# Software-issued weight-sum transfers released by an attention counter, and key transposes without a holding time

## The chip, the core and the metric

The kernel runs on one core of a Trainium2 chip. The metric is the device time of one execution in microseconds (us), taken as the median of three runs. A profile of one more execution gives, for each engine, when every instruction began and how long it took. Engines are called as in the profile: PE is TensorE's matmul, PEld its weight load, DVE VectorE, ACT ScalarE, POOL GpSimd, SP SyncE. An engine with a q behind its name (SPq, POOLq) is its queue.

## What is computed

One decoder block on 512 tokens of width 1024, in float32. The input is normalised and projected into fifteen pieces; two token mixers run beside each other; their outputs are gated, merged, projected, normalised and added to the input.

```python
h = rms_norm(x, norm_pre)
proj = h @ w_in
(q_n, k_c, v_c, k_s, v_s, k_w, v_w, g_n, z_n,
 q_r, k_r, v_r, z_r, m_a, m_b) = jnp.split(proj, split_points(), axis=-1)
...
y_a = (o_a * jax.nn.silu(z_n)) @ w_nsa_o      # o_a: sparse attention, 8 heads of 64
...
y_b = (o_b * jax.nn.silu(z_r)) @ w_ret_o      # o_b: retention, 4 heads
merged = jax.nn.sigmoid(m_a) * y_a + jax.nn.sigmoid(m_b) * y_b
x = x + rms_norm(merged @ w_out, norm_post)
```

The attention has three branches with softmaxes of their own: keys compressed by a small network (`cmp_w1`, `cmp_w2`), selected keys and a sliding window.

## The kernel before

**Precision.** Every float32 operand of a large product is split into a rounded high part and the rest (`whi`, `wlo` for weights, `hTh`, `hTl` for the normalised input, `kA`, `kB` for keys), and a product is three matmuls: high by high, high by low, low by high. ACT or DVE makes the high part, DVE the low part (`sub_split`, which is a subtraction in `tt`, line 209).

**Weights.** They lie in one stream in the order of their use. SP loads them in pieces of 512 KB into four buffers `raw` (`load_next`, line 354); `splitter` makes `whi`/`wlo` halves of 512 columns from them into nine buffers; a `raw` buffer is loaded anew when both halves are split. Each piece holds two contraction steps of 128 (two "kt").

**Stages of `main`.** First the block A (the keys and values of the compressed and selected branches, 512 columns, four token tiles t at once), then block C (280 columns: window keys, values and gates; one tile after the other, eight kt of three matmuls each), then the queries Q (tiles 3, 2, 1, 0), then the two halves of the compression network (`hidden(0)`, `hidden(1)`: four pieces of weights each), then the blocks of `PLAN`, of which Z is the first (four passes over the same four pieces of weights). Attention runs between the matmuls of Q to ZR, retention between those of the blocks VR.

**What sets the order.** No queue is sorted by the hardware. The body is a set of Python generators; `Order.run` picks the next one by priority and by a clock of its own, which adds up estimated costs (`self.now` for PE, `self.eng` for the others). A generator that yields a number isn't resumed before that time on the planner's clock, one that yields a function not before the function is true. What an instruction waits for on the chip is set by its data alone: a time that was yielded is not in the program.

**Keys of block A (`tail_a`, lines 589 to 619).** For each tile t: ACT scales the product out of PSUM into `nat`; DVE turns it (`rope16`) and copies each key twice into `kd` (`doubled`, line 564, 128x768); then `keysT` makes PE transpose two 128x128 pieces of `kd` (line 234, `ident`), ACT writes `kA` and DVE `kB`; then four more transposes with `identp` feed `Xk` and `Xv` (four additions on DVE), the input of the compression network. There are two buffers for `kd`, and two PSUM banks (91 and 92) for transposes. Between the copy and `keysT` the generator yields `e + HOLD`, with HOLD 1500 ns. Block C's keys go the same way (`tail_c`, 128x256 copies, `arena_l`), without a holding time.

**Weight sums (`weight_sums`, lines 327 to 337).** The two blocks of `SEVEN` (the second halves of the gates m_a and m_b) are multiplied with seven products in place of eight, which needs sums of weight blocks. They are made in DRAM by 16 transfers of 512 KB that POOL issues through the software queue: eight copies out of the weight stream (line 334), then eight with `accum_op=OP.add` (line 336), of which the first four add from the stream and the last four add one sum to another (`t<-t`). The accumulating ones wait for the transfers that wrote their operands. The sums are read as weights from 383 us on. In the planner the k-th transfer is yielded at 110 us + k times 12 us.

**The gated products (`att_sum`, lines 920 to 942).** When the eighth part of an output (t, g) of the attention is there, the branches' sum is multiplied into `szn` by `tt(...)`, which by its default runs on DVE; then a flag `att{t}{g}` is set in the planner. Eight such flags make `ATT`.

**POOL's other work** in the middle of the kernel: four additions `gate` (one for each tile of block C), eight powers `rv` in retention (line 209), and four `rr` at the end.

Of the kernel before, what the change touches and what calls it, by code (L numbers as in the profile page):

```python
# [36 lines left out]
ISSUE = 8.0  # L37
SLACK = 700.0
WAKE = 7
HOLD = 1500.0  # L40
T0, TSTEP = 110000.0, 12000.0
DVE_BIAS = 400


# [95 lines left out]
def block_kernel(ctx: ExitStack, tc, x, xT, x0s, ws, small, w2s, norm_post, rope_r, dmask, out):  # L140
# [19 lines left out]
    def at(kb, n, dt=FT):  # L160
        o = int(kb * 256)
        if dt == FR:
            return arena_r[:, o:o + n]
        assert o >= 28 * 256 or o + n <= 28 * 256
        return arena_f[:, o - 28 * 256:o - 28 * 256 + n] if o >= 28 * 256 else arena_l[:, o:o + n]
# [30 lines left out]
    def act(o, i, func=AF.Copy, r=0.0, **kw):  # L196
        S.activation(o, i, func, **kw)  # L197
        return od.op("act", act_ns(o, i, lazy(kw.get("bias"), kw.get("scale"))) + (95 if "accum_out" in kw else 0), r)
# [9 lines left out]
    def tt(o, a, b, op, r=0.0, e="dve"):  # L208
        (V if e == "dve" else G).tensor_tensor(o, a, b, op=op)  # L209
        if op == OP.pow:  # L210
            return od.op(e, 300 + 164 * size(o), r, True)
        return od.op(e, (1.042 * size(o) + 69) if e == "dve" else (2.36 * size(o) + 77), r, e == "pool" or near(o, a, b))
# [20 lines left out]
    def tr(ps, a, idn, r=0.0):  # L233
        T.transpose(ps, a, idn)  # L234
        return od.pe(86 if a.dtype == FR else 108, r, 45.0 if a.dtype == FR else 31.0)
# [75 lines left out]


    loads, off = [], 0
    sums = []
    for pieces in stream_shape():
        if pieces == "seven":
            b11, b12, b21, b22 = (ws[off + i * P * 1024:off + (i + 1) * P * 1024].rearrange("(p n) -> p n", p=P)
# [9 lines left out]
    def weight_sums():  # L327

        for n in range(8):
            for i, block in enumerate(sums):  # L330
                yield T0 + TSTEP * (n * len(sums) + i)
                o, a = block[n]
                if n < 4:
                    G.dma_start(o, a)
                else:
                    G.dma_start(o, a, accum_op=OP.add)
                od.op("pool", 900.0)
# [186 lines left out]
    def rs(t, i=0):  # L524
        return rs3[:, i, t:t + 1]
# [16 lines left out]
    def rope16(v, t, shape, r, e="dve"):  # L542

        n = int(np.prod(shape))
        pat = {1: "p (a c) -> p a c", 2: "p (a b c) -> p a b c"}[len(shape)]
        kw = dict(zip("ab", shape))
        t1, t2 = (at(41 + 0.5 * i, n * 16).rearrange(pat, **kw) for i in range(2))

        def bc(a):
            c = a.shape[-1]  # L550
            for _ in shape:
                a = a.unsqueeze(1)
            return a.broadcast_to([P, *shape, c])
        ix = (slice(None),) * (1 + len(shape))
        lo, hi, al = ix + (slice(0, 8),), ix + (slice(8, 16),), ix + (slice(0, 16),)
        tt(t1, v[al], bc(ropen[:, t, 0:16]), OP.mult, r, e)
        tt(t2[lo], v[hi], bc(ropen[:, t, 16:24]), OP.mult, r, e)
        r = tt(t2[hi], v[lo], bc(ropen[:, t, 24:32]), OP.mult, r, e)
        return tt(v[al], t1, t2, OP.add, r, e)

    def doubled(kn, a, b, kd, r):

        n = (b - a) // 64
        V.tensor_copy(kd.rearrange("p (a r c) -> p a r c", a=n, r=2),
                      kn[:, a:b].rearrange("p (a c) -> p a c", c=64).unsqueeze(2).broadcast_to([P, n, 2, 64]))
        return od.op("dve", 0.53 * n * P + 70, r, True)

    def keysT(kd, off, br, t, r):
        ps = yield from PT.get()
        yield r + PE_LAG  # L570
        for g in range(2):
            e = tr(ps[:, g * P:(g + 1) * P], kd[:, off + g * P:off + (g + 1) * P], ident, r)
        yield e, "act"
        v = ps[:, 0:256].rearrange("p (g c) -> p g c", g=2)
        sl = (slice(None), br, slice(None), slice(t * P, (t + 1) * P))
        e = act(kA[sl], v, r=e)
        yield e, "dve"
        e = sub_split(kB[sl], v, kA[sl], e)
        PT.put(ps, e)
        return e  # L580

    def vals(src, br, t, r):
        for g in range(2):
            sv = src[:, g * 64:(g + 1) * 64]
            e = act(VS[:, t, br, g, g, :], sv, r=r)
            e = sub_split(VS[:, t, br, g, 1 - g, :], sv, VS[:, t, br, g, g, :], e)
        return e

    def tail_a(t, ps, e, ring):
        yield od.need("const", "rs")  # L590
        kn = yield from NAT.get()
        yield max(e, constr["rope"], rsr[0]), "act"
        e = act(kn, ps, r=e, scale=rs(t))
        ring.put(ps, e)
        yield e, "dve"
        v = kn.rearrange("p (b e) -> p b e", b=2)[:, :, 0:128].rearrange("p b (g c) -> p b g c", g=2)
        e = rope16(v, t, (2, 2), e)
        kd = yield from KD6.get()
        e = doubled(kn, 0, 384, kd, e)
        ev = vals(kn[:, 384:512], 0, t, 0.0)  # L600
        NAT.put(kn, ev)
        yield e + HOLD
        yield from keysT(kd, 512, 0, t, e)
        pc = yield from PT.get()
        yield e + PE_LAG
        for i in range(4):
            ep = tr(pc[:, i * P:(i + 1) * P], kd[:, i * P:(i + 1) * P], identp, e)
        KD6.put(kd, ep)
        yield ep, "dve"
        for i, X in enumerate((Xk, Xv)):  # L610
            src = pc[:, i * 256:(i + 1) * 256].rearrange("p (g l c) -> p g l c", g=2, l=16)
            for hf in range(2):
                rr = slice(hf * 64, hf * 64 + 64)
                c0 = 8 * t - hf
                lo = 1 if c0 < 0 else 0
                o = X[rr, :, :, c0 + lo:c0 + 8].rearrange("p l g c -> p g l c")
                ep = tt(o, src[rr, :, :, lo:8],
                        pes[i][rr, :].unsqueeze(1).unsqueeze(3).broadcast_to([64, 2, 16, 8 - lo]), OP.add, ep)
        PT.put(pc, ep)
        od.flags.add(f"A{t}")  # L620
# [291 lines left out]
    def att_out():  # L912
        for t, g in ((t, g) for t in reversed(range(NT)) for g in range(2)):
            yield lambda: (t, g) in avs
            a = avs[t, g]
            po = yield from PO.get()
            a["po"] = po
            od.spawn(att_sum(t, g, po), 1)

    def att_sum(t, g, po):  # L920
        a = avs[t, g]
        yield lambda: a["n"] == a["total"]
        yield od.need("Z0", "Z1", "Z2", "Z3")
        m, o = slice(g * 64, g * 64 + 64), slice(64 - g * 64, 128 - g * 64)
        low = yield from NAT.get()
        yield a["e"], "act"
        e = act(low[m], po[o], r=a["e"])
        yield e, "dve"
        e = tt(low[m], po[m], low[m], OP.add, e)
        PO.put(po, e)  # L930
        yield e, "pool"
        gv = szn[m, :, t * P:(t + 1) * P]
        e = tt(gv, low[m].rearrange("p (j c) -> p j c", j=4), gv, OP.mult, e)
        NAT.put(low, e)
        od.flags.add(f"att{t}{g}")
        if all(n in od.flags for n in ATT):
            DMA.dma_start(dm, dmask.rearrange("h p c -> p h c"))
            dmr.append(od.dma(P * 2048, a["e"]))
            for o in (32, 36):
                VR[0].put((at(o, 512, FR), at(o + 2, 512, FR)))  # L940
            for _ in range(2):
                b = yield from PO.get()
                PS.put(b)
# [530 lines left out]
    od.spawn(splitter(), lambda: rank(nxt[0])())  # L1474
    od.spawn(edges(), 1)
    od.spawn(weight_sums(), 1)
    od.spawn(main(), MAIN)
    od.run()
# [28 lines left out]
def stream_shape():  # L1507

    yield [512, 512]
    yield from [[1024]] * 3  # L1510
    yield from [[560]] * 4
    yield from [[1024]] * (4 + 8)
    for b in PLAN:
        yield from ["seven"] if b in SEVEN else [[1024]] * (2 if b[0] == "NO" else 4)
    yield from [[1024]] * 8
# [67 lines left out]
```

## Time and profile before

| | |
|---|---|
| median of three runs | 528.15 us (527.85 to 531.55) |
| profiled execution, its own time | 528.24 us |
| its span, first to last instruction | 526.5 us |
| mean granted clock of PE | 0.997 |
| PE busy | 514.9 us (98% of the span) |
| DVE, ACT, POOL busy | 405.6, 290.5, 23.8 us |
| read, written in HBM | 66.26 MB, 10.49 MB |

The span has 1.7 us less than the time of that execution. Matmuls overlap: one of 512 columns is shown with some 0.39 us, and the next one starts 0.23 us behind it. So starts are compared here, and not durations. A row of the timeline gives the start, the duration, the engine and line, what was done, and in brackets the idle time ahead of it with what ended that. In the list of transfers the last column is the time from issue to landing.

### The profile page before, as it was taken

The numbers are of one execution on the slowest core, as the hardware profiler recorded it, in microseconds if no ns is written. First come the engines' busy times: TensorE is split into PE (matmuls) and PEld (weight loads), VectorE is DVE, ScalarE is ACT, GpSimd is POOL, SyncE is SP. The second block draws the span as 40 slices with busy tenths as digits, with TensorE's granted clock in tenths as the row PEclk, the third lists the DMA queues.
The fourth block names the chain that finished last, engine by engine and source line by source line (L and its number), as shares of the span: only waits on it lengthen the run. The fifth ranks groups of instructions, "written<-read, shape, count | busy, mean of one in ns | idle before, by whom it ended". The sixth has DMA issues, their size and how long they took to land.

```text
span 526.5 us, 7843 instructions
## 1 busy us (share of the span) xinstructions
PE 514.9 (98%) x2778; PEld 440.8 (84%) x2778; DVE 405.6 (77%) x980; ACT 290.5 (55%) x627; POOL 23.8 (5%) x48
## 2 busy tenths in 40 slices
PE   8989999999999999999999999999999999999995
PEld 7888888788888888888878888888788989988884
DVE  6698799989979889997886576786889867645533
ACT  6663798768557886784525353524557434323411
POOL 1002100000000000000111000000000000000000
PEclk9999999999999999999999999999999999999998
DMA  8956769601304004133543532141643726625032
GB/s 311 365 198 200 220 132 260 209 2 40 121 1 129 33 0 156 36 112 119 109 136 66 190 125 76 41 120 42 219 141 122 237 83 202 205 114 159 1 109 92
DMA packets 22456, 68.87 MB, mean 131 GB/s; under 512 B 2448, under 2 KB 3728, under 8 KB 22416
## 3 DMA queue, kind: packets, MB, share of 16 engines
q1 hardware_dynamic: 19968, 59.84, 33.9%
q0 software_dynamic: 2304, 8.39, 7.2%
q8 instruction: 22, 0.36, 0.3%
q10 hardware_dynamic: 144, 0.14, 0.1%
q14 instruction: 18, 0.15, 0.1%
HBM read 66.26 MB, written 10.49 MB: 146 GB/s over the span
## 4 chain that ended last, share of the span: by engine, by line
PE 81%; DVE 7%; DMA 7%; issue 2%; ACT 1%; SPq 1%; POOLq 0%; DVEq 0%; POOL 0%; ACTq 0%
PE bank L230 76%; DMA raw<-in_stream_dram 6%; PE bank L234 6%; DVE wlo L209 3%; DVE arena_r L209 1%; DMA arena_f<-in_xT_dram 1%; DVE arena_l L844 1%; DVE arena_f L209 1%; DVE arena_l L218 1%; ACT whi L197 0%; DVE nat L209 0%; ACT arena_l L197 0%; DVE whi L205 0%; SPq L477 0%; DVE arena_f L222 0%
## 5 line engine op out<-in xcount | busy, mean ns | idle before, releaser
L197 ACT ACTIVATE whi<-raw 128x512 fp32r<-128x512 f32 x159 | 95.7, 626 | 41.3 <-PE bank L230 32.2
L209 DVE TENSOR_TENSOR wlo<-raw,whi 128x512 fp32r<-128x512 f32 x172 | 111.7, 685 | 7.6 <-ACT whi L197 6.8
L230 PE MATMUL bank<-whi,hTh 128*128 128x512 f32 x256 | 99.7, 405 | 0.8 <-DVE arena_r L222 0.4
L230 PE MATMUL bank<-whi,hTl 128*128 128x512 f32 x256 | 96.2, 391 | 0.0
L230 PE MATMUL bank<-wlo,hTh 128*128 128x512 f32 x256 | 96.1, 391 | 0.0
L230 PE MATMUL bank<-arena_r 128*128 128x256 f32 (+2 forms) x328 | 70.7, 336 | 0.3 <-DVE arena_r L209 0.3
L230 PE MATMUL bank<-arena_r,whi 128*128 128x512 f32 (+1 forms) x208 | 63.8, 382 | 0.7 <-DVE sg L222 0.7
L197 ACT ACTIVATE arena_r<-bank 128x512 fp32r<-128x512 f32 (+2 forms) x80 | 45.2, 570 | 29.1 <-PE bank L234 27.7
L197 ACT ACTIVATE arena_l<-arena_l,stat 128x128 f32<-128x128 f32 (+3 forms) x104 | 55.3, 552 | 5.6 <-DVE stat L209 2.7
L209 DVE TENSOR_TENSOR arena_r<-bank,arena_r 128x512 fp32r<-128x512 f32 (+2 forms) x72 | 46.8, 656 | 13.8 <-ACT arena_r L197 13.1
L230 PEld LDWEIGHTS bank<-whi,hTl 128*128 128x128 f32 x256 | 48.0, 188 | 10.6
L230 PEld LDWEIGHTS bank<-arena_r 128*128 128x128 f32 x328 | 51.0, 189 | 6.5 <-DVE arena_r L209 0.6
L230 PEld LDWEIGHTS bank<-whi,hTh 128*128 128x128 f32 x256 | 48.0, 188 | 9.5 <-DVE arena_r L222 0.9
L230 PEld LDWEIGHTS bank<-wlo,hTh 128*128 128x128 f32 x256 | 48.3, 189 | 8.2
L230 PE MATMUL bank<-hTh,whi 128*128 128x512 f32 (+1 forms) x144 | 52.4, 364 | 0.0
L230 PE MATMUL bank<-hTh,wlo 128*128 128x512 f32 (+1 forms) x144 | 51.2, 355 | 0.0
L230 PE MATMUL bank<-hTl,whi 128*128 128x512 f32 (+1 forms) x144 | 51.1, 355 | 0.0
L230 PE MATMUL bank<-whi,arena_r 128*128 128x512 f32 (+1 forms) x176 | 48.7, 352 | 0.0
L230 PEld LDWEIGHTS bank<-arena_r,whi 128*128 128x128 f32 x208 | 38.8, 188 | 8.6 <-DVE sg L222 1.3
L230 PE MATMUL bank<-arena_r,wlo 128*128 128x512 f32 x96 | 37.4, 389 | 0.0
L230 PEld LDWEIGHTS bank<-whi,arena_r 128*128 128x128 f32 x176 | 32.1, 189 | 4.6
L230 PE MATMUL bank<-wlo,arena_r 128*128 128x512 f32 (+1 forms) x104 | 34.7, 343 | 0.3 <-DVE wlo L209 0.3
(164 smaller groups left out, 768.4 us busy)
## 6 DMA issues: line engine op xcount, KB each, us to landing
raw<-in_stream_dram SPq DMA_DIRECT2D x77, 512.0 KB, 4.3
t<-in_stream_dram POOLq DMA_DIRECT2D x12, 512.0 KB, 5.3
raw<-t SPq DMA_DIRECT2D x8, 512.0 KB, 3.7
arena_f<-in_rope_r_dram SPq DMA_DIRECT2D x8, 256.0 KB, 2.7
t<-t POOLq DMA_DIRECT2D x4, 512.0 KB, 5.4
arena_f<-in_xT_dram SPq DMA_DIRECT2D x8, 256.0 KB, 3.7
ends<-in_x_dram SPq DMA_DIRECT2D x4, 512.0 KB, 5.5
arena_l<-in_xT_dram SPq DMA_DIRECT2D x7, 256.0 KB, 5.7
```

Source lines behind the costliest of these rows:

```text
L197: S.activation(o, i, func, **kw)
L209: (V if e == "dve" else G).tensor_tensor(o, a, b, op=op)
L218: V.tensor_scalar(o, a, s1, s2, op0=op0, op1=op1)
L230: T.matmul(ps, a, b, start=start, stop=stop)
L234: T.transpose(ps, a, idn)
L844: V.tensor_tensor_reduce(pv[:, b, :], sv[:, b, :], maskp[:, 512 - L:512], 1.0, -NEG, OP.add, OP.min, nm[:, b:b + 1])
```

## The change

It has two parts. The times at which the planner releases the 16 software transfers are replaced by a counter: transfer k is released when k is below twice the number of finished outputs of the attention (`PER = 2`; eight outputs release 16 transfers). And the holding time between the copy of block A's keys and their transposes is dropped.

```diff
-HOLD = 1500.0
-T0, TSTEP = 110000.0, 12000.0
+PER = 2
...
-    sums = []
+    sums, atts = [], [0]
...
         for n in range(8):
             for i, block in enumerate(sums):
-                yield T0 + TSTEP * (n * len(sums) + i)
+                while (n * len(sums) + i) >= PER * atts[0]:
+                    yield lambda: (n * len(sums) + i) < PER * atts[0]
                 o, a = block[n]
                 if n < 4:
                     G.dma_start(o, a)
...
         ev = vals(kn[:, 384:512], 0, t, 0.0)
         NAT.put(kn, ev)
-        yield e + HOLD
         yield from keysT(kd, 512, 0, t, e)
...
         od.flags.add(f"att{t}{g}")
+        atts[0] += 1
```

No instruction is added or removed: PE has 2051 rows in the order of both, POOL the same 16 transfers, four additions and twelve powers. What moves is their order. Lines of the changed kernel are one lower from line 42 to 328 and from 603 to 935, so lines 229, 233 and 208 there are 230, 234 and 209 before.

**POOL behind the first eight transfers.** `t_115` to `t_122` are the eight sums in DRAM, `rv` are retention's powers. Before:

```order
L336 DMA t_115<-in_stream_dram 128x1024
L336 DMA t_119<-in_stream_dram 128x1024
L336 DMA t_117<-in_stream_dram 128x1024
L336 DMA t_121<-in_stream_dram 128x1024
L209 TENSOR_TENSOR rv<-rv,nhalf 128x2
L336 DMA t_116<-t_117 128x1024
L209 TENSOR_TENSOR rv<-rv,nhalf 128x2
L336 DMA t_120<-t_121 128x1024
L209 TENSOR_TENSOR rv<-rv,nhalf 128x2
L336 DMA t_118<-t_116 128x1024
L209 TENSOR_TENSOR rv<-rv,nhalf 128x2
L336 DMA t_122<-t_120 128x1024
```

The changed kernel:

```order
L336 DMA t_115<-in_stream_dram 128x1024
L336 DMA t_119<-in_stream_dram 128x1024
L336 DMA t_117<-in_stream_dram 128x1024
L336 DMA t_121<-in_stream_dram 128x1024
L336 DMA t_116<-t_117 128x1024
L336 DMA t_120<-t_121 128x1024
L336 DMA t_118<-t_116 128x1024
L336 DMA t_122<-t_120 128x1024
L208 TENSOR_TENSOR rv<-rv,nhalf 128x2 x8
```

The last four transfers stood each behind one of the powers; now all 16 follow each other, and all eight powers stand behind them. Ahead of the 16 stand the four additions `gate` in both; no gated product of the attention is in this queue.

**PE in block C.** `bank_87` and `bank_88` collect block C's tiles (tile 0 ends in the first row), `arena_f` is `kd` of block A, `arena_l` that of block C. Before:

```order
L230 MATMUL bank_87<-arena_r,hTl 128x280
L230 MATMUL bank_88<-arena_r,hTh 128x280 x2
L230 MATMUL bank_88<-arena_r,hTl 128x280
...
L234 MATMUL bank_91<-ident,arena_f 128x128 x2
...
L230 MATMUL bank_87<-arena_r,hTl 128x280
L234 MATMUL bank_92<-ident,arena_l 128x128 x2
...
L234 MATMUL bank_91<-identp,arena_f 128x128 x4
```

The changed kernel:

```order
L229 MATMUL bank_87<-arena_r,hTl 128x280
L233 MATMUL bank_91<-ident,arena_f 128x128 x2
L229 MATMUL bank_88<-arena_r,hTh 128x280 x2
L229 MATMUL bank_88<-arena_r,hTl 128x280
...
L233 MATMUL bank_92<-ident,arena_f 128x128 x2
...
L233 MATMUL bank_91<-identp,arena_f 128x128 x4
```

The first pair of transposes stood behind three kt (nine matmuls) of tile 1 and now stands ahead of them; the second pair of block A now follows three kt later; the first pair of block C (`arena_l`), which came second, has moved into the queries, some 60 matmuls on.

**DVE around the last copies of block C's keys.** `arena_r<-arena_l` and `arena_r<-arena_f` of 128x16x64 are the low parts of `Xk` and `Xv`. The changed kernel:

```order
L208 TENSOR_TENSOR arena_r<-arena_l,arena_r 128x16x64
L564 COPY arena_l<-nat_110 128x256
L208 TENSOR_TENSOR arena_r<-nat_110,arena_r 128x64 x2
L208 TENSOR_TENSOR arena_r<-bank_92,arena_r 128x2x128
L208 TENSOR_TENSOR arena_r<-arena_f,arena_r 128x16x64
L564 COPY arena_l<-nat_112 128x256
```

Before, all four copies of 128x256 stand ahead of these two subtractions.

From there on the order of PE, DVE and ACT differs in small moves through the attention; from row 1161 of 2051 on PE's order is the same but for the names of buffers.

## Prediction

> **What bounds the kernel now.** I read the page's busy times and the chain that ended last, then each engine's busy time by stretches (start and end in us, the length, then the busy time of PE, PEld, DVE, ACT and POOL, PE's clock, the DMA engines' share, GB/s).
>
> ```profile
> PE 514.9 (98%) x2778; PEld 440.8 (84%) x2778; DVE 405.6 (77%) x980; ACT 290.5 (55%) x627; POOL 23.8 (5%) x48
> PE 81%; DVE 7%; DMA 7%; issue 2%; ACT 1%; SPq 1%; POOLq 0%; DVEq 0%; POOL 0%; ACTq 0%
> 27.00:42.60 15.60, 13.70 (x108) 13.27 (x107) 14.95 (x60) 10.20 (x29) 0.76 (x3) 1.00 0.45 159
> 42.60:62.00 19.40, 19.40 (x106) 16.01 (x105) 15.27 (x45) 9.43 (x20) 5.45 (x10) 1.00 0.83 260
> 62.00:80.00 18.00, 17.68 (x103) 14.94 (x102) 17.02 (x52) 16.79 (x37) 2.05 (x3) 1.00 0.64 143
> 80.00:100.00 20.00, 19.49 (x117) 16.30 (x116) 18.44 (x38) 15.54 (x35) 0.42 (x1) 1.00 0.88 261
> 100.00:245.00 145.00, 145.00 (x765) 122.29 (x764) 130.65 (x378) 104.92 (x257) 0.00 (x0) 1.00 0.22 72
> 245.00:300.00 55.00, 54.56 (x282) 46.02 (x281) 39.70 (x88) 23.16 (x43) 6.56 (x8) 1.00 0.46 117
> 300.00:516.00 216.00, 215.27 (x1165) 186.43 (x1164) 147.96 (x280) 91.60 (x172) 4.35 (x7) 1.00 0.38 123
> ```
>
> PE is the bound: from 27 to 516 us its idle times are 1.90, 0, 0.32, 0.51, 0, 0.44 and 0.73, 3.9 us in sum. The change adds no matmul and takes none away, and neither the start nor the tail moves, so it can gain some 4 us at the most and lose whatever new waits it makes. A measurement of this kernel tells a change of about 1% (5.3 us) from none; a gain of that size isn't there to be had. The question is what waits the new order makes, in two places.
>
> **First part: the key transposes.** PE's timeline in block C:
>
> ```profile
> 29.71 0.43 PE L230 MATMUL bank<-arena_r,hTh 128*128 128x280 f32 x2
> 30.74 0.29 PE L230 MATMUL bank<-arena_r,hTl 128*128 128x280 f32 x1
> 32.04 0.41 PE L234 MATMUL bank<-ident,arena_f 128*128 128x128 f32 x2 [1.01 <-DVE arena_f L564]
> 34.85 0.29 PE L230 MATMUL bank<-arena_r,hTl 128*128 128x280 f32 x1
> 36.04 0.44 PE L234 MATMUL bank<-ident,arena_l 128*128 128x128 f32 x2 [0.90 <-DVE arena_l L564]
> ```
>
> and DVE's copies, with one of the two subtractions of 1024 columns:
>
> ```profile
> 31.34 0.56 DVE L564 COPY arena_f<-nat 128x768 f32<-128x768 f32 x1
> 32.79 0.56 DVE L564 COPY arena_f<-nat 128x768 f32<-128x768 f32 x1
> 54.93 1.22 DVE L209 TENSOR_TENSOR arena_r<-arena_l,arena_r 128x1024 fp32r<-128x1024 f32 x1
> ```
>
> A matmul of 280 columns takes a step of 0.13, so two starts came late: 32.04 against 30.87 (1.17) and 36.04 against 34.98 (1.06). Both waited for a copy. DVE's order up to the copies is unchanged, and PE started 0.14 behind the copy's end (31.90).
>
> In the changed order the first pair stands where tile 1 begins, at 29.71, and still can't start before 32.04: a wait of 2.33, since three kt that covered part of it now come behind it. The second pair comes 0.26 + 9 x 0.13 us later, at about 33.45; its copy ends at 33.35, PE can start at 33.49: 0.05. The pair of block C has moved so far back that its wait is gone. So far 2.33 + 0.05 - 1.17 - 1.06 = +0.15.
>
> Then DVE. Between the first copy of block C and its last one the changed order has all sixteen additions into Xk and Xv (0.41 each) and both subtractions of 1024 columns (1.15 from start to start). I added DVE's work from 40.7, where the low part of tile 2's keys ends: 13.1 us of it, and about 1.4 of waits for ACT's halves of Xk and of the values, put the last copy's end at 55.2. PE, with 42 matmuls of 512 columns (0.23 each) and eight pairs of transposes (0.2) from 43.35 on, wants it at 54.65. That is a wait of 0.7. With an error of a microsecond in either sum it is 0 to 1.7. The first part costs 0.15 + 0.7, say **+0.8**; bounds 0 and +1.8. What hides the rest: attention's first scores stand at 61.5 in both.
>
> **Second part: the transfers.** The flag of the counter is one of the planner; the product in front of it runs on DVE, and POOL has no wait for it. So POOL issues all 16 in a row as fast as their own queue lets it. How fast is that?
>
> ```profile
> 43.41 0.26 POOL L209 TENSOR_TENSOR gate<-nat,cst 128x24 f32<-128x24 f32 x1 [3.29 <-ACT nat L197]
> 59.83 0.85 POOL L336 DMA_DIRECT2D t<-in_stream_dram  x1 [3.45 <-issue]
> 65.41 0.84 POOL L336 DMA_DIRECT2D t<-in_stream_dram  x1 [4.73 <-issue]
> 73.98 0.81 POOL L336 DMA_DIRECT2D t<-in_stream_dram  x1 [7.74 <-issue]
> 79.59 0.83 POOL L336 DMA_DIRECT2D t<-in_stream_dram  x1 [4.80 <-issue]
> ...
> 250.07 0.86 POOL L336 DMA_DIRECT2D t<-t  x1
> ```
>
> The landings of those issued at 59.83, 65.41, 73.98 and 250.07, each from the list of transfers of its moment:
>
> ```profile
> t<-in_stream_dram POOLq DMA_DIRECT2D x1, 512.0 KB, 5.3
> t<-in_stream_dram POOLq DMA_DIRECT2D x1, 512.0 KB, 8.3
> t<-in_stream_dram POOLq DMA_DIRECT2D x1, 512.0 KB, 5.3
> t<-t POOLq DMA_DIRECT2D x1, 512.0 KB, 5.2
> ```
>
> Each accumulating transfer is issued 0.3 us behind the landing of the one before: 59.83 + 5.3 = 65.1 and 65.41; 65.41 + 8.3 = 73.7 and 73.98; 73.98 + 5.3 = 79.3 and 79.59. The fourth (79.59) took 8.2, below, and lands at 87.8. Before, POOL then stood still until the first power of retention, and the next was issued at 250.07. Now the fifth goes out at 88.1, or at 88.9, since the last gate's addition, ahead of all 16, comes about 0.8 later (block C ends at 43.35 in place of 42.58, the six transposes that were moved ahead into it included). It runs to about 96, the sixth to about 103, and two more until 115.
>
> There the loads of weights run close behind each other. The landing times of the fourth (issued at 79.59) and of the load issued just ahead of it (79.40), then the DMA queues' shares from 82 to 86 and from 86 to 102, then the chain of waits, with the times of two later loads from issue to landing (7.29 and 4.29):
>
> ```profile
> t<-in_stream_dram POOLq DMA_DIRECT2D x1, 512.0 KB, 8.2
> raw<-in_stream_dram SPq DMA_DIRECT2D x1, 512.0 KB, 3.2
> ...
> q0 software_dynamic: 130, 0.48, 67.1%
> q1 hardware_dynamic: 42, 0.13, 33.5%
> ...
> q1 hardware_dynamic: 1268, 4.60, 82.7%
> ...
> 81.82 7.29 DMA raw<-in_stream_dram
> 89.79 1.38 DVE wlo L209 x2
> 91.20 4.29 DMA raw<-in_stream_dram
> 95.58 0.64 ACT whi L197
> 96.85 0.68 DVE wlo L209
> ```
>
> One accumulating transfer took the DMA engines for most of 82 to 86, and the load beside it landed after 7.29 in place of 4.29: 3.0 us late, and those behind it with it, because each load queues behind the last. Without it (86 to 102) the loads alone fill 83%. The four loads of Z land in that stretch, the last at 95.50, and its low part ends at 97.5, with PE on it. So 3.0 us come through to PE, less what the new order puts between Z's second and last kt: the compression network's two small products and two matmuls of attention, which took 0.47 and 0.55 before. 3.0 - 1.0 = 2.0. POOL's start 0.8 later also lets the fourth transfer end later, on which the last load of `hidden(1)` hangs; half of that, 0.4. Together **+2.4**. Bounds: 0, if the fifth lands so late or Z's loads so early that they miss each other, and 2 x 3.0 = 6.0, if the sixth also gets ahead of Z's last load. The sixth to eighth meet only the loads of the next block, which PE wants three passes of Z (17 us) later, or none.
>
> **What is taken away late.** At 250 to 286 four transfers leave. The loads there were not held up much:
>
> ```profile
> raw<-in_stream_dram SPq DMA_DIRECT2D x1, 512.0 KB, 3.3
> raw<-in_stream_dram SPq DMA_DIRECT2D x1, 512.0 KB, 3.4
> 269.43 0.50 PE L230 MATMUL bank<-whi,hTh 128*128 128x512 f32 x1 [0.44 <-DVE arena_r L222]
> ```
>
> (loads issued at 257.14 and 264.37). PE's one wait there is for DVE, which had seven low parts of weights ahead of what PE needed; in the changed order seven still stand there. So 0, between -0.7 and +1. The moves inside the attention I also take as 0: PE has no idle time from 100 to 245, with DVE busy for 130.65 of 145, so there are 14 us of cover; without that cover one or two waits like those at 80 to 100, up to +2.
>
> **Sum.** 528.24 (that execution; 0.09 above the median) + 0.8 + 2.4 + 0 = **531.4 us**, 0.6% more and within 1%.
>
> **The rivals.**
>
> *No collision.* The fifth transfer comes later than Z's loads. Then 528.24 + 0.8 = 529.0. For it: Z's stretch may begin earlier on PE, or POOL be held. Against it: the issue of each transfer followed its predecessor's landing within 0.3 us, and there are no reasons in the order for POOL to stop. [...]
>
> *Two ahead of Z (slower).* If Z's loads are held up by the fifth for more than some 2 us, the sixth is issued while the last of them is still out, and takes its 3.0 too: 528.24 + 0.8 + 0.4 + 6.0 - 1.0 = 534.4. The point from which this decides: the fifth lands before Z's last load is through, which in the forecast is 96 against 98.5. For it: that is already so by 2 us. Against it: packets of the sixth first move 1 to 2 us after its issue, and loads already queued go first (the load issued at 79.40, just before a transfer, took 3.2).
>
> *The walk of block C is wrong.* The planner's new order removes both old waits and makes none in their place, and the late wait at 269 goes as well: 528.24 - 2.2 - 0.7 = 525.3. Against it: the copy ends at 31.90 whatever PE does.
>
> **How the numbers follow.** Forecast 0.52, no collision 0.22, two ahead of Z 0.20, waits removed 0.06. The forecast's own range is 529.7 to 533. The range to 8 in 10 takes in no collision below and two ahead of Z above, with its bounds (1.8 for block C, some of the 2 in the attention): **527.0 to 536.5**. Slower by over 1% (above 533.4): most of the third case and a little of the first, 0.22. Faster by over 1% (below 522.9): only by more than all of PE's waits, 0.03. Within 1%: 0.75.
>
> **What would show it.** In the profile after: one wait of about 2.2 us for `arena_f` L564 at 32 us, none for it or `arena_l` at 36, and one of about 0.7 near 55; four rows `t<-t` on POOL between 88 and 115; loads at 88 to 96 that take 6 to 8 us and PE waiting for `wlo` between 90 and 100 for 2 us more than before; powers `rv` with no transfers between them. If PE's idle time at 80 to 100 is as it was, the second term is wrong; if it sums to more than 5, the third case holds; if there are waits between 100 and 245, the cover of the attention is what I misjudged.

## The result, and the profile after

| | before | changed |
|---|---|---|
| median | 528.81 us | 533.22 us |
| mean | 528.95 us | 533.76 us |
| lowest to highest, 22 runs each | 527.49 to 531.55 us | 529.24 to 540.34 us |
| ratio to before, 95% interval | | 1.0068, 1.0050 to 1.0087 |
| profiled execution, span | 528.24, 526.5 us | 530.62, 528.8 us |

The ratio is 1.0068 and the medians' quotient 1.0083, since the ratio leaves out runs more than 1.5% above the fastest of their kernel, here the four above 537.2 us, without which the changed kernel's mean is 532.6. The changed kernel is slower by 0.5 to 0.9%, within the 1% of the forecast. Two things stand out. The median is 1.8 us above the forecast of 531.4: just outside the forecast's own range (529.7 to 533), inside the wider one (527.0 to 536.5). And the changed kernel's runs scatter by 3.2 us (standard deviation) where those of before scatter by 1.0. The profiled execution is one of its quick ones, and by itself it doesn't tell where the slower ones lose.

Busy times by stretches in the changed kernel's profile, in the columns of the prediction's first table:

```profile
27.00:42.60 15.60, 13.32 (x106) 13.02 (x105) 14.50 (x59) 9.70 (x28) 0.70 (x3) 1.00 0.50 168
42.60:62.00 19.40, 19.40 (x108) 15.86 (x107) 16.17 (x46) 8.94 (x20) 4.56 (x9) 1.00 0.74 254
80.00:100.00 20.00, 19.05 (x114) 15.38 (x113) 16.12 (x32) 14.57 (x32) 1.73 (x3) 1.00 0.95 262
100.00:245.00 145.00, 144.77 (x756) 121.61 (x756) 130.73 (x381) 103.84 (x258) 1.65 (x2) 1.00 0.28 83
245.00:300.00 55.00, 55.00 (x289) 46.92 (x288) 40.61 (x89) 25.13 (x47) 3.11 (x4) 1.00 0.25 85
```

PE's idle time (length less PE's busy time) is 2.28 us at 27 to 42.6 (1.90 before), none at 42.6 to 62, 0.95 at 80 to 100 (0.51 before), 0.23 in the long attention stretch and none at 245 to 300 (0.44 before). The DMA engines' share at 80 to 100 rose from 0.88 to 0.95, that at 245 to 300 fell from 0.46 to 0.25: the four transfers have moved. PE's wait in block C, and the changed kernel's POOL from the fourth accumulating transfer on:

```profile
32.83 0.41 PE L233 MATMUL bank<-ident,arena_f 128*128 128x128 f32 x2 [2.28 <-DVE arena_f L564]
```

```profile
79.25 0.83 POOL L336 DMA_DIRECT2D t<-in_stream_dram  x1 [4.95 <-issue]
86.39 0.82 POOL L336 DMA_DIRECT2D t<-t  x1 [6.32 <-issue]
95.51 0.83 POOL L336 DMA_DIRECT2D t<-t  x1 [8.29 <-issue]
102.59 0.82 POOL L336 DMA_DIRECT2D t<-t  x1 [6.25 <-issue]
110.13 0.82 POOL L336 DMA_DIRECT2D t<-t  x1 [6.71 <-issue]
```

One wait in place of two in block C, and four `t<-t` in a row at 86 to 110 that stood between the powers before. The list of transfers for 84 to 102 us shows what the weight loads (`raw`) have beside them:

```profile
q1 hardware_dynamic: 994, 3.64, 55.9%
q0 software_dynamic: 346, 1.22, 39.9%
...
raw<-in_stream_dram SPq DMA_DIRECT2D x7, 512.0 KB, 6.2
t<-t POOLq DMA_DIRECT2D x2, 512.0 KB, 7.8
```

The software queue takes 40% of the DMA engines there, and seven loads have a median of 6.2 us from issue to landing.

### The profile page after: what moved, and what is told of

It is laid out like the page before. It is cut to its first block, busy times and chain, and to the rows that moved or that the text cites. A ratio compares the mean times of both kernels' runs of the same rounds, so it can differ in the third digit from the quotient of the medians.

```text
span 528.8 us, 7840 instructions
## 1 busy us (share of the span) xinstructions
PE 516.3 (98%) x2778; PEld 440.6 (83%) x2778; DVE 404.9 (77%) x981; ACT 289.7 (55%) x628; POOL 23.6 (4%) x48
## 4 chain that ended last, share of the span: by engine, by line
PE 83%; DMA 8%; DVE 4%; issue 2%; ACT 2%; SPq 0%; POOL 0%; POOLq 0%; DVEq 0%; ACTq 0%
PE bank L229 77%; PE bank L233 6%; DMA raw<-in_stream_dram 3%; DMA arena_l<-in_x_dram 2%; DMA arena_l<-in_xT_dram 2%; DVE wlo L208 1%; DMA arena_f<-in_xT_dram 1%; ACT arena_l L196 1%; DMA x<-in_x_dram 1%; ACT whi L196 1%; DVE arena_l L843 1%; DVE arena_r L208 0%; DVE arena_l L217 0%; DVE nat L208 0%; DVE arena_f L208 0%
## 5 line engine op out<-in xcount | busy, mean ns | idle before, releaser
L208 DVE TENSOR_TENSOR wlo<-raw,whi 128x512 fp32r<-128x512 f32 x172 | 112.2, 686 | 7.7 <-ACT whi L196 6.1
L196 ACT ACTIVATE whi<-raw 128x512 fp32r<-128x512 f32 x158 | 94.5, 626 | 42.2 <-PE bank L229 31.8
L196 ACT ACTIVATE arena_l<-arena_l,stat 128x512 f32<-128x512 f32 (+3 forms) x106 | 56.8, 559 | 6.0 <-DVE stat L225 2.8
L208 DVE TENSOR_TENSOR arena_r<-bank,arena_r 128x512 fp32r<-128x512 f32 (+2 forms) x72 | 46.7, 656 | 15.0 <-ACT arena_r L196 14.4
```

## The experiments

The span of the profiled execution grew by 2.3 us, the mean of all runs by 4.8. To follow both, the table has beside each kernel's mean time the mean of its runs' granted clocks, how many runs had a clock below 0.9955, and the mean of time multiplied by clock. That product is about the time that an execution would have had with the full clock throughout: the profiles below show the clock at half for a spell of 3.4 us, or two (a clock of 0.51 for 3.40 us in e2, 0.50 for 6.70 us in e11), and a spell costs half its length, an estimate of 1.7 us from these rows, if PE has work in it. (The profiled executions before and after also end at half clock behind PE's last work, for 3.5 and 1.9 us. That costs no time, and it lowers the product by 1.8 and 0.9 us.) The standard errors of the products are 0.1 to 0.6 us, so a difference of less than some 0.8 us between two of them isn't shown.

| | mean us | clock | below 0.9955 | us x clock | ratio to before, 95% |
|---|---|---|---|---|---|
| before, 24 runs (with e1 to e4) | 528.7 | 0.9973 | 2 of 24 | 527.3 | |
| before, 34 runs (with e5 to e8) | 528.6 | 0.9976 | 1 of 34 | 527.3 | |
| changed kernel | 533.8 | 0.9940 | 16 of 22 | 530.5 | 1.0050 to 1.0087 |
| its 18 runs that the ratio counts | 532.6 | 0.9951 | 12 of 18 | 530.0 | |
| e1 transfers alone | 531.6 | 0.9970 | 1 of 10 | 530.0 | 1.0037 to 1.0079 |
| e2 order alone | 530.9 | 0.9939 | 7 of 9 | 527.6 | 1.0024 to 1.0066 |
| e3 changed, less last four | 530.9 | 0.9951 | 7 of 12 | 528.3 | 1.0027 to 1.0067 |
| e4 behind the products | 535.0 | 0.9918 | 6 of 6 | 530.7 | 1.0094 to 1.0159 |
| e5 old order, all behind Z | 527.7 | 0.9971 | 0 of 12 | 526.2 | 0.9976 to 0.9999 |
| e6 new order, all behind Z | 527.6 | 0.9962 | 6 of 12 | 525.6 | 0.9966 to 0.9999 |
| e7 changed, fill at 32 | 533.6 | 0.9947 | 8 of 11 | 530.8 | 1.0064 to 1.0124 |
| e8 new order, behind Z, fill | 526.9 | 0.9976 | 0 of 12 | 525.6 | 0.9963 to 0.9987 |

### The two parts apart (e1, e2)

The changed order of PE, DVE and ACT comes from the dropped holding time alone, and POOL's changed order from the counter alone, so the two parts can be had one at a time. e1 is the kernel before with the counter:

```diff
-                yield T0 + TSTEP * (n * len(sums) + i)
+                while (n * len(sums) + i) >= PER * atts[0]:
+                    yield lambda: (n * len(sums) + i) < PER * atts[0]
```

> The transfers' part alone: the holding time of 1500 ns stays, so PE, DVE and ACT have the order of before row by row, and POOL has that of the changed kernel (all 16 transfers in a row, the powers behind them). Theory (collision: the last four accumulating transfers now run at 86 to 115 us, against the loads of hidden(1) and Z): 530.5 to 533 us beside 528.8, ratio 1.004 to 1.008, with runs that differ more among themselves than those of before, and PE idle at 80 to 100 us for 1.5 us or more beside 0.5. Rival (the new order of PE, DVE and ACT costs the time, the transfers nothing): 528.8, ratio 0.999 to 1.001.

Median 531.67 us (528.76 to 534.22), ratio 1.0058, as the theory had it. Its profile, an execution of 534.22 and the slowest of the ten, shows where that one lost:

```profile
93.93 0.50 PE L230 MATMUL bank<-hTh,whi 128*128 128x512 f32 x1 [1.37 <-ACT whi L197]
102.88 0.63 ACT L197 ACTIVATE whi<-raw 128x512 fp32r<-128x512 f32 x1 [3.92 <-DMA raw<-in_stream_dram]
103.55 0.69 DVE L209 TENSOR_TENSOR wlo<-raw,whi 128x512 fp32r<-128x512 f32 x1 [2.81 <-ACT whi L197]
...
104.76 0.68 DVE L209 TENSOR_TENSOR arena_r<-bank,arena_r 128x512 fp32r<-128x512 f32 x1
105.49 0.44 PE L234 MATMUL bank<-ident,arena_f 128*128 128x128 f32 x2 [2.15 <-DVE arena_r L209]
```

Read upwards from the last row: PE waits 2.15 us for a low part that belongs to the attention. Ahead of it on DVE stands the low part of a weight, for which DVE waited for ACT's half, and ACT waited 3.92 us for a load to land. That load, issued at 95.23 beside the fifth accumulating transfer (out from 93.29 to 101.53), took 7.57 us. It isn't one of Z's: counted in the stream it is the 25th piece, the first of block MA (A, C, Q and Z have four pieces each, the compression network eight), which PE itself needs much later. The wait of 1.37 us is for Z's first load, issued at 84.82 beside the fourth transfer (83.86 to 92.97), which took 8.35 us. Accumulating transfers hold up loads here, as the second term of the prediction has it, but neither wait is the one that it priced, of Z's loads for the fifth. This is also the one run of ten with a lowered clock: it is at half from 106.7 to 110.1, behind the wait of 2.15.

e2 is the kernel before without the holding time; the transfers keep their old release times:

```diff
-HOLD = 1500.0
...
-        yield e + HOLD
```

> The holding time's part alone: it is dropped, the times 110 us + 12 us k stay, so PE, DVE and ACT have the order of the changed kernel row by row and POOL that of before (the last four transfers each behind a power of retention). Theory: block C's walk gives +0.2 to +0.8, so 529.0 to 529.6 us, ratio 1.000 to 1.002, no more spread than before; a wait of 2.3 us for the copy at 32 us. Rival (the order costs the time): 532, ratio 1.005 to 1.009.

Median 530.55 us (529.67 to 533.14), ratio 1.0045: above the theory's 529.0 to 529.6, below the rival's 532. Seven of nine runs had a lowered clock. Its timeline has two waits of some 2 us:

```profile
32.03 0.41 PE L233 MATMUL bank<-ident,arena_f 128*128 128x128 f32 x2 [2.04 <-DVE arena_f L563]
...
86.46 0.43 DVE L204 CAST whi<-raw 128x512 fp32r<-128x512 f32 x1 [2.52 <-DMA raw<-in_stream_dram]
86.81 0.68 DVE L208 TENSOR_TENSOR wlo<-raw,whi 128x512 fp32r<-128x512 f32 x1
...
87.41 0.68 DVE L842 CUSTOM_DVE_ANT_0 arena_l<-bank,maskp 128x512 f32<-128x512 f32 x1
88.02 0.08 DVE L842 DVE_READ_ACCUMULATOR2_ANT stat<- 128x1 f32 x1
...
88.15 0.72 PE L229 MATMUL bank<-arena_r 128*128 128x512 f32 x2 [1.75 <-DVE stat L842]
```

and PE's clock is down behind the first of them, in the stretch from 32.4 to 35.8 us:

```profile
32.40:35.80 3.40, 3.40 (x17) 3.39 (x16) 3.12 (x18) 2.72 (x10) 0.23 (x1) 0.51 0.58 218
```

PE is busy in all of these 3.4 us, at a clock of 0.51. The chain of waits has the load that the second one goes back to:

```profile
80.07 6.30 DMA raw<-in_stream_dram
```

It is a wait of place in a queue: in the new order a row of the attention's scores (L842) stands on DVE behind the split of a weight (L204, L208) whose load, issued just behind the fourth accumulating transfer, lands only at 86.4. Nothing in the scores needs that weight. The load is the third of `hidden(1)`, and the fourth transfer is none of those that the change moves: the kernel before has it too, but in its profile the load was issued 0.2 us ahead of it (79.40 and 79.59) and landed after 3.2 us, and here it was issued 0.5 us behind it.

In time multiplied by clock the parts cost +2.7 (e1) and +0.3 us (e2), together 3.0, and the whole change +3.2 (+2.7 by the 18 runs); the 0.3 is within the scatter. What is lost to the lowered clock, the mean time less that product, is 1.4 us before, 1.6 in e1, 3.2 in e2 and 3.2 in the changed kernel (2.6 by the 18 runs). That the last two are near each other is partly chance: e7 and e9 to e12 show that the changed kernel loses it mostly at another place.

### The last four transfers left out (e3)

```diff
-                else:
+                elif n < 6:
                     G.dma_start(o, a, accum_op=OP.add)
```

> The changed kernel with the last four accumulating transfers (one sum added to another) left out of POOL's queue and nothing else changed; four of the eight sums are therefore incomplete. Theory: this takes away the collision and leaves the order: 529.0 to 529.8 us, ratio 1.000 to 1.002, spread as before, loads at 86 to 96 us landing after 4 to 5 us. Rival (order): as the changed kernel, 532, ratio 1.005 to 1.009.

Median 531.18 us (528.22 to 533.21), ratio 1.0047: above the 529.0 to 529.8 that were expected, and like e2, as it should be if the last four cost what the changed kernel has above e2. In time multiplied by clock they cost 530.5 - 528.3 = 2.2 us here (1.7 by the 18 runs), and 530.0 - 527.3 = 2.7 in the old order (e1).

### Transfers that really stand behind the products (e4)

A one-column copy on POOL of each gated product makes the counter bind on the chip:

```diff
+        G.tensor_copy(seen[m, 0:1], szn[m, 0, t * P:t * P + 1])
         od.flags.add(f"att{t}{g}")
         atts[0] += 1
```

> The changed kernel with the wait that its counter only has in the planner: behind each gated product POOL copies one column of it (64x1), so that two transfers are released by each of the eight outputs on the chip too, and all 16 move into the attention, some 120 to 260 us. Theory (any transfer of the software queue beside loads that PE hangs on costs time): the first twelve leave 45 to 87 us as well, PE's idle time at 62 to 100 falls under 1 us, 527.5 to 529 us, ratio 0.997 to 1.000, small spread. Rival (order): 531.5 to 532.5, ratio 1.005 to 1.008. A third possibility: the transfers slow the loads of the attention's stretch or POOL's copies hold DVE, then ratio over 1.002 with PE idle between 120 and 260.

535.02 us (532.04 to 538.10), the slowest of all, where the theory had 527.5 to 529. The stretch of Z is clean now, its only idle PE gone:

```profile
80.00:102.00 22.00, 22.00 (x133) 18.98 (x132) 20.64 (x47) 17.25 (x37) 0.00 (x0) 1.00 0.72 239
```

but the transfers now end late, and a power that retention needs stands behind the last of them:

```profile
256.77 0.82 POOL L337 DMA_DIRECT2D t<-t  x1 [4.62 <-issue]
257.66 0.73 POOL L208 TENSOR_TENSOR rv<-rv,nhalf 128x2 f32<-128x2 f32 x1
258.42 0.99 DVE L217 TENSOR_SCALAR arena_l<-bank,mv,rv 128x256 f32<-128x256 f32 x2 [6.03 <-POOL rv L208]
261.01 1.11 PE L233 MATMUL bank<-ident,arena_l 128*128 128x128 f32 x4 [4.67 <-DVE arena_l L208]
```

So a software transfer can cost time in two places: beside the loads of 80 to 105 us, and ahead of retention's powers. The next two kernels put all sixteen between the two.

### All sixteen behind Z's loads, in both orders (e5, e6)

One column of the compressed keys, written at about 100 us, is copied on POOL ahead of all sixteen. e5 is the kernel before with that, e6 the changed kernel:

```diff
+        yield od.need("cmp0")
+        G.tensor_copy(seen[:, 0:1], f(kc[:, 0, 0, 0:1]))
+        od.op("pool", 65.0)
         for n in range(8):
             for i, block in enumerate(sums):
-                yield T0 + TSTEP * (n * len(sums) + i)
+                yield
```

> The kernel before with all sixteen transfers of the weight sums held in GpSimd's queue behind a one-column copy of the compressed keys, which are written at about 100 us: PE, DVE, ACT and SP keep the order of the kernel before, the transfers run from about 102 to 195 us, where few loads are (DMA share 0.21 before). Theory A (the transfers cost by delaying Z's loads between 80 and 105 us; the reordering costs by a longer wait near 32 us, after which TensorE's clock is at half for 3.41 us in some executions): the 0.5 us of idle PE at 80 to 102 us goes, 527.3 to 528.1 us against 528.6, clock 0.997 as before. Theory B (the reordering costs because DVE and ACT, in their new order, stand behind a load that a transfer delays): the same here. Rival C (what the transfers cost does not depend on where they lie): 528.6 or more, with new waits at 102 to 195 us.

> The same place for the sixteen transfers, and the changed kernel's order on PE, DVE and ACT. Theory A: the wait near 32 us is 2.2 to 2.9 us as in the changed kernel, so the runs' mean clock falls from 0.997 to about 0.994 and the mean time lies 1.5 to 2.2 us above the run with the order before; time multiplied by clock is within 0.5 us of it. Theory B: with no transfer beside Z's loads the wait of 1.9 us near 86 us is gone, the mean time is within 0.5 us of the run with the order before and the clock 0.997.

e5: 527.74 us (526.75 to 528.64), 0.9 below the kernel before; that the cost doesn't depend on the place is out. Its sixteen transfers run from 99 to 164 us. e6: 527.72 us (525.85 to 529.45), and the expectation that it lies 1.5 us or more above e5 failed; in time multiplied by clock the new order is 0.7 us lower, about as much as the scatter allows. But it has a lowered clock in 6 of 12 runs, which e5 has in none, and these six average 528.8 us against 526.3 of the other six. e6's profile has the wait at 32 us and the spell behind it:

```profile
32.64 0.41 PE L233 MATMUL bank<-ident,arena_f 128*128 128x128 f32 x2 [2.00 <-DVE arena_f L567]
```

```profile
33.90:37.20 3.30, 3.30 (x17) 3.29 (x16) 2.89 (x19) 1.88 (x8) 0.23 (x1) 0.50 0.33 129
```

The wait near 86 us is gone with the transfers: PE's waits in e6's profile have none over 0.5 us between 33 and 370 us. With no transfer beside the loads, then, the new order costs nothing that is clear of the scatter but the clock at 32, which e6 has in half of its runs.

### Filling the idle stretch at 32 us (e7, e8)

```diff
+        if t == 0 and br == 0:
+            for _ in range(8):
+                T.transpose(ps[:, 0:P], ident, ident)
         for g in range(2):
             e = tr(ps[:, g * P:(g + 1) * P], kd[:, off + g * P:off + (g + 1) * P], ident, r)
```

> The changed kernel's order with the sixteen transfers behind the compressed keys, and the eight filling transposes near 32 us. Theory A: mean clock 0.997, mean time within 0.5 us of the run with the order before and the same transfers, 527.3 to 528.3 us. Theory B: the same as without the filling transposes, whatever that is.

> The changed kernel, with eight transposes of the identity (about 0.2 us each) put in PE's order right ahead of the two key transposes that wait near 32 us; they write a bank that those overwrite, and nothing else moves. They shorten the idle stretch there from 2.3 to about 0.7 us without ending the wait sooner. Theory A: fewer executions with a lowered clock, mean clock 0.9965 or more in place of 0.994, mean time 1.3 to 2 us below the changed kernel's 533.8. Theory B: nothing changes, 533 to 534 us with a mean clock of 0.994.

e8, which is e6 with the fill: 526.87 us (525.55 to 528.37), no run of 12 with a lowered clock, where e6 had six, and a little below the 527.3 to 528.3 expected. Its ratio to the kernel before is 0.9975 (0.9963 to 0.9987): it is faster than both kernels. The eight transposes do nothing but keep PE busy, for 1.04 us of the wait in e7's profile. In e8's own profile there is no wait to fill: PE comes to the transposes only at 32.39 us, 2.3 later than in e7's, since it had begun more slowly (9 matmuls between 7 and 10 us, where the kernel before has 15). So what the fill does is read from the twelve runs, and the length of the wait at 32 differs between executions: 0.3 us in e9, which began as slowly, 2.6 in e3.

e7, the changed kernel with the fill, was a miss of theory A: 534.04 us (528.95 to 537.17), 8 of 11 runs with a lowered clock, as without it. In the changed kernel, then, the clock is mostly lost somewhere else than at 32 us.

### Four slower executions (e9 to e12)

Three more profiles of the changed kernel (e9 to e11), and one of e7's kernel (e12).

> The changed kernel once more, for the profile of another execution: the first, of 530.6 us, showed no lowered clock and was among the fastest. Three theories of where its slower executions lose: A, at the wait near 32 us (2.2 to 2.9 us of idle PE, then 3.41 us at half clock); D, between 85 and 115 us, where loads stand beside the four last accumulating transfers: waits of 1.5 us or more there, the lowered clock right behind one; F, somewhere after 250 us. An execution of 533 us or more tells them apart, one of 531 or less does not.

> As the look before: A, the lowered clock at 32 to 36 us; D, between 85 and 115 us, behind a wait of 1.5 us or more; F, after 250 us.

> As the two looks before: A, the lowered clock at 32 to 36 us; D, between 85 and 115 us, behind a wait of 1.5 us or more; F, after 250 us.

> The changed kernel with the eight filling transposes near 32 us once more, for another execution than the profiled one of 528.95 us: its mean of 533.6 us and mean clock of 0.9947 were no better than without them. A: idle PE at 32 us of 1.5 us or more all the same, and the lowered clock there. D: no lowered clock at 32 to 36 us; waits of 1.5 us or more and the lowered clock between 85 and 115 us. F: after 250 us.

They took 533.80, 535.03, 535.02 and 533.03 us: all slower executions than the profiled one, and all four lose between 84 and 109 us. e9 first, with POOL, ACT, DVE and PE around its one long wait:

```profile
78.57 0.83 POOL L336 DMA_DIRECT2D t<-in_stream_dram  x1 [4.79 <-issue]
...
87.57 0.43 DVE L204 CAST whi<-raw 128x512 fp32r<-128x512 f32 x1 [4.07 <-DMA raw<-in_stream_dram]
...
87.92 0.68 DVE L208 TENSOR_TENSOR wlo<-raw,whi 128x512 fp32r<-128x512 f32 x1
...
88.52 0.68 DVE L843 CUSTOM_DVE_ANT_0 arena_l<-bank,maskp 128x512 f32<-128x512 f32 x1
89.13 0.08 DVE L843 DVE_READ_ACCUMULATOR2_ANT stat<- 128x1 f32 x1
...
89.26 1.22 PE L229 MATMUL bank<-arena_r 128*128 128x512 f32 x2 [3.30 <-DVE stat L843]
```

This is e2's second wait, with 3.30 us in place of 1.75; the chain of waits has the load behind it:

```profile
79.64 7.84 DMA raw<-in_stream_dram
```

e11 lost more, 20 us later. Its chain, its PE, and its stretches around the lowered clock:

```profile
93.60 8.56 DMA raw<-in_stream_dram
...
102.24 0.64 ACT whi L196
...
102.91 0.69 DVE wlo L208
103.60 0.61 DVE arena_r L208
```

```profile
104.25 0.80 PE L229 MATMUL bank<-arena_r 128*128 128x512 f32 x1 [3.85 <-DVE arena_r L208]
```

```profile
102.40:109.10 6.70, 4.85 (x11) 3.80 (x12) 5.81 (x19) 3.09 (x7) 0.70 (x1) 0.50 0.65 141
109.20:113.00 3.80, 3.80 (x23) 3.23 (x22) 1.15 (x5) 1.76 (x5) 0.82 (x1) 1.00 0.26 25
```

The load issued at 93.60 takes 8.56 us here: the sixth accumulating transfer was out beside it, from 92.62 to 101.97. It is again the first load of MA (its counterpart before took 4.48; Z's last, issued at 92.41, took 3.81), and again DVE has the split of a weight that isn't needed yet ahead of the low part that PE waits for. PE waits 3.85 us, and the clock is at half from 102.4 to 109.1, two spells. e10 has two spells, one from 33.4 on, behind the wait at 32, and one from 105.1 on, at the end of a wait of 2.3 us with the same chain behind it (MA's first load, issued at 95.89, took 7.19):

```profile
33.40:36.70 3.30, 3.30 (x16) 3.29 (x15) 2.90 (x17) 2.27 (x9) 0.23 (x1) 0.50 0.53 204
36.80:40.00 3.20, 3.20 (x27) 3.20 (x27) 2.87 (x11) 0.90 (x3) 0.23 (x1) 1.00 0.00 0
...
105.10:108.30 3.20, 3.13 (x7) 2.49 (x8) 3.03 (x14) 2.21 (x4) 0.00 (x0) 0.50 0.95 207
```

and e12, with the fill, none at 32 and one at 87.3 to 90.6, which begins inside a wait of 2.55 us:

```profile
87.75 1.22 PE L229 MATMUL bank<-arena_r 128*128 128x512 f32 x2 [2.55 <-DVE stat L846]
```

Of the six half-clock spells in these four executions (the two that follow each other in e11 counted as two), five lie at 87 to 109 us and one at 33; none lies after 250. For comparison, the loads in e8's list of transfers for 80 to 97 us, where no software transfer is out:

```profile
raw<-in_stream_dram SPq DMA_DIRECT2D x9, 512.0 KB, 4.3
```

4.3 us, where the changed kernel's profile has 6.2.

## Why the prediction was right in its number, and where it was not

**The bound, and the class.** PE is the bound and the change lies within 1% of before: right. The sum of the two terms, +3.2 us, is what time multiplied by clock grew by (527.3 to 530.5; 2.7 by the 18 runs). That is luck in part, since the terms are not what it is made of, as the next points show. The measured mean grew by 4.8 to 5 (3.7 by the 18 runs); the rest is the lowered clock, a term that the working doesn't have.

**First part, +0.8: the step that failed.** The wait of 2.33 us at 32 is there (2.28 idle, 2.56 from start to start), the one at 36 is gone, and PE's idle time in the stretch rose by 0.38 where 0.15 was worked out. The wait of 0.7 near 55 us is not there: PE is busy for all of 42.6 to 62 in every profile, so the sum over DVE's work by hand was too long. What failed is that the working put two waits of 1.17 and 1.06 us on the same scale as one of 2.33. They are not the same: behind the two short ones the clock stayed at 1.00 in the profile before, behind the long one it fell to half for 3.4 us in a share of the executions (e2, e6, e10), and with the same order and the transposes in the wait it fell in none of twelve runs (e8). With no transfer beside the loads this is some 0.7 us on the mean (2.0 lost to the clock in e6, 1.3 in e8); in e2 it is 1.8, more than twice the whole term, of which the wait at 88 may have a part.

**"Moves inside the attention", 0 with up to +2.** The cover was read from 100 to 245 us. There it held in e2, e6 and the profile after (0, 0.07 and 0.23 us idle) and not in e10 and e11, whose waits at 104 and 105 us lie in it. Nor did it hold ahead of it, at 84 to 89, where the new order put a row of scores on DVE behind the split of a weight that wasn't there yet: 0.54 us in the profiled execution after, 1.75 in e2 and 3.30 in e9. That is within the bound given, and not the value taken. It takes the order and a transfer beside the load: with the transfers behind Z (e6) the same order has no such wait. The transfer is the fourth, which the change doesn't move. The working gave it 0.4 us, since it would end later; in the profile after it ended earlier (86.08 and 87.79), and what it held up was the load that is now issued behind it, 5.1 to 7.8 us in the changed kernel's profiles and 3.2 before.

**Second part, +2.4: the size came out, the path did not.** In time multiplied by clock the last four transfers cost 2.7 in the old order and 1.7 to 2.2 in the new one. POOL did what was said: all sixteen in a row with no wait for the products, and each accumulating transfer 0.3 us behind the landing of the one before; the fifth went out at 86.39 (88.1 to 88.9 forecast) since the fourth took 6.8 in place of 8.2. Z's loads were held up too: its second took 8.47 us beside the fifth transfer in the profile after. But where 2.0 us of waiting for them was taken, PE waited 0.38 us there, 0.24 in e9, 0.75 in e12 and not at all in e10 and e11, and its idle time at 80 to 100 went from 0.51 to 0.95. The step that failed is the sentence that the sixth to eighth transfers "meet only the loads of the next block, which PE wants three passes of Z (17 us) later". PE does want them later, but DVE has the split of that block's first weight in its queue ahead of a low part of the attention, and for that PE waited 2.15 us in e1 (beside the fifth), 2.29 in e10 and 3.85 in e11 (beside the sixth). These are slower executions, and what the last four cost in a middling one has its size shown and its path not. As far as the traces go, another wait stood in place of the priced one, and that the sum still came out is luck.

**Two ahead of Z, 534.4 at 0.20.** Its condition was met in e9 and e12: there the sixth was issued at 95.15 and 91.98, ahead of Z's last load at 96.03 and 94.40, which took 5.74 and 6.24 us in place of 4.29. Its price wasn't: PE waited 0.24 and 0.75 us for that load, and those executions took 533.8 and 533.0 us mostly by other waits (3.30 and 2.55 us at 85 to 90) and a spell. That one kernel has executions with different waits, in place of one outcome of several, is what the list of cases missed; the scatter of 3.2 us goes with it.

**No collision, and waits removed.** Both out: e1 alone costs 2.7. POOL was not held beside a busy DVE: the changed kernel's transfers went out 0.3 us behind each landing at 80 to 100 us, with DVE busy for 16.12 of 20 us there, as before at 62 to 80 us with 17.02 of 18.

**Taken away late, 0 (-0.7 to +1).** PE's idle time at 245 to 300 went from 0.44 to 0: a gain of 0.4, within the bounds.

**What the clock records settle, and what stays open.** PE was idle for 2.57 us at 27 to 42.6 us in e3's profile and the clock stayed at 1.00, while waits of 2.0 us at 32 us had it at half behind them in e2 (2.04), e6 (2.00) and e10 (2.0). The rows for 28 to 36 us, e2's first and then e3's:

```profile
28.00:32.00 4.00, 1.99 (x16) 1.77 (x15) 3.86 (x12) 3.71 (x9) 0.00 (x0) 1.00 0.92 302
32.00:36.00 4.00, 3.97 (x20) 3.99 (x21) 3.69 (x23) 3.17 (x12) 0.23 (x1) 0.57 0.58 219
...
28.00:32.00 4.00, 1.93 (x16) 1.71 (x14) 3.93 (x11) 3.81 (x9) 0.00 (x0) 1.00 0.91 313
32.00:36.00 4.00, 3.50 (x28) 3.50 (x29) 3.76 (x22) 3.53 (x13) 0.23 (x1) 1.00 0.67 245
```

Up to 32 us PE was busy for nearly the same time, 1.99 us in e2 and 1.93 in e3, and only e2's clock fell. So the wait costs the clock in some executions only (6 of 12 of e6's runs have it lowered), and its length alone doesn't decide; what else does was not shown. Eight transposes, 1.04 us of work in e7's profile, would lift e2's 1.99 us to 3.0 (an estimate from these rows), and e8's twelve runs have none with a lowered clock. It also stays open what share of the changed kernel's lowered clock each of the places has, since four executions are few, and why e6's runs with a lowered clock lose more than one spell costs.

## What to carry to other kernels

Where PE is the bound, weigh one long wait more than two short ones of the same sum (here 2.0 us had the half clock behind it in three profiles, and the 1.01 and 0.90 us of the profile before had not): read the granted clock right behind every wait of some 2 us, in more than one execution, and if the wait can't be had away, fill it with work that PE can do at once. PE stood idle for 2.28 us at 32 us in the profile after with three kt behind the two transposes in its order, and for 3.85 us in e11 since DVE had a weight's split ahead of the low part. So a reordering, or a transfer that delays a load, is judged by what stands on every engine behind the operand that comes late, at the place where transfers are densest, and not by when PE needs that operand or by the mean cover of the stage. A transfer that nobody needs for a long time belongs where the queues are idle: tie it with a small operation on its own engine to something that is written there, since a planner's flag ties nothing on the chip.

## What the runs showed of the hardware

The granted clock had a price for a wait here on top of its length: e6's six runs with a lowered clock are 2.5 us slower than its other six, where one spell accounts for 1.7 (the estimate above). The scatter goes with it: of the 18 runs that the ratio counts, the changed kernel's average 530.5 us at a clock of 0.9955 or more (6 runs), 533.0 at 0.9935 to 0.9955 (6) and 534.5 below that (6). Waits of 2.0 us at 32 us were followed by the half clock in e2, e6 and e10; one of 2.28 us in the profiled execution after wasn't.

The transfers that accumulate in DRAM slowed more than their own queue. One of 512 KB took 5.1 to 9.4 us in the changed kernel's four profiles, one was out at a time, and loads of 512 KB in the other queue beside the last four landed after 3.8 to 8.6 us, with a median of 6.2 in the profile after, in place of 4.3 in e8. The two queues had 40% and 56% of the same 16 DMA engines there, so what GpSimd issued bore on when SyncE's loads landed.
